# A third set of query and key tiles with loads two heads ahead, and the samples' 8x8 systems inverted on TensorE

## The chip, the cores and the metric

The kernel runs on one NeuronCore of one Trainium2 chip. Its time is the device time of one execution in microseconds (us), and smaller is better. Three runs of the kernel before took 1567.76 to 1576.21 us, with a median of 1574.98 us.

## What is computed

One step of a one-layer decoder for a prompt of 1024 tokens and for 8 samples of 8 tokens each, all float32 in and out:

```
h = rmsnorm(x); P = h @ w_in                      # RWKV columns, then q, k, v
RWKV-7: 8 heads of 64, a recurrence over the tokens, group norm, gate
attention: 8 heads of 64; scores = q k^T / 8 - slope * distance, three
           dilated windows (128,1), (512,4), (2048,16), softmax, @ v; rmsnorm
x = x + concat(rwkv, attention) @ w_out
x = x + top-2 of 8 experts in the best of 4 groups   # 32 gated MLPs of 1024x256
x = x + (p @ w_ple) * sigmoid(rmsnorm(x) @ w_ple_gate); y = rmsnorm(x)
```

The recurrence per head is `s = s*w - (s kk)(kk*a)^T + v k^T`, `y = s r`. In the blocked form it needs, for each block of tokens, the inverse of a unit triangular matrix, T = (I - A)^-1, where A is strictly triangular. For the samples a block is 8 tokens, so A is eight 8x8 blocks on a 64x64 diagonal for each head, and A to the eighth power is zero.

## The kernel before, in words

The program is written as phases on one core, and a scheduler lays the instructions of all phases out on the five engines before the run: each engine then works through its own fixed list in order, and an instruction that waits holds up all that stand behind it in the list. Loads that SyncE (SP) issues also wait for the transfer eight places earlier in its list.

Phase 1 projects all tokens. Phase 2 runs the prompt's recurrence in eight units of 128 tokens, phase 3s the samples' attention over the caches, mixed with phase 2. Phase 3 is the prompt's attention: for each of eight heads and each block `i` of 128 queries, `pS` (q times k, in pieces of 512 keys, L1040), a bias and a maximum on VectorE (L1043), exp on ScalarE (L1052), transposes `pxt` (L1063) and `po` (times v, L1069). Heads 0 and 1 are done in two goes: blocks 0 to 4 in a first call of `phase3`, blocks 5 to 7 in a second, which then does heads 2 to 7 whole. Between the two calls stands the code of phase 2s, the samples' recurrence, whose instructions the scheduler mixes into the attention. Phase 4 multiplies by w_out (`p4y`, L1289) and routes, phase 5 is the experts, phase 6 the end.

A head's k and q come in by `head` (L971, L974): GpSimd (POOL) issues three transfers, k once and q as a high and a low part. The tiles come from the pool `qk3` with two buffers for each name, and `phase3` calls `head` for the unit at hand and the next one. So the load of head h+1 waits until the last `pS` of head h-1 has read its tiles. The bias table of the head (L976, on SP) has two buffers too and is loaded in the same function.

In phase 2s, `prepA` forms the products that hold A in the tile `LAB` (L618) and writes them to memory (`ABs`, L620). `solve_s` (L728) reads the diagonal 8x8 blocks back with eight small loads (L737), inverts all 64 of them by substitution on VectorE (seven pairs of L742 and L744), writes the result into a zeroed array in memory (L748, L750) and reads it back as the tile `TTs` (L752). `sample2` uses `TTs` in `pus` (L820), behind `pst`, `pws` and `pas`.

`attn_out` (L902) takes a finished block of 128 queries: a square with its sum (`asq`, ScalarE, L908), the root on VectorE and POOL (`arm`, `arr`), the scaled rows (`an`, VectorE, L911), four transposes (`pxo`, TensorE, L914), a copy (`ao`, ScalarE, L916) and a store to `MX` (SP, L917), from where phase 4 reads it (L1331). `asq`, `an` and `ao` have one buffer each. The single PSUM bank of `pxo` is used by `p4h`, the routing product of phase 4, after the eighth block.

Of the kernel before, what the change touches and what calls it, by code (L numbers as in the profile page):

```python
# [10 lines left out]
F32 = mybir.dt.float32  # L11
F32R = mybir.dt.float32r
# [9 lines left out]
NP = 1024  # L22
# [438 lines left out]
class K2(K):  # L461
# [10 lines left out]
    def dram2(self):  # L472
        t = lambda n, s: self.dp.tile(s, F32, name=n)
        self.MX = t("MX", [8, 128, T])
        self.ABd = t("ABd", [8, 2, 2, 8, 32, 32])
        self.ABs = t("ABs", [8, 64, 64])
        self.XZ = t("XZ", [8, 64, 64])

    def pools2c(self, es):

# [117 lines left out]
    def prepA(self, u):  # L598

        nc = self.nc  # L600
        smp = u == 's'
        nck, t0, n = (1, NP, 64) if smp else (2, 128 * u, 128)
        ch = self.ch[0 if smp else u // 2 % 2]
        R = lambda t: ch.tile([128, nck, 4, 128], F32, tag=t, name=t)
        G = dict(AR=ch.tile([128, 4, nck, 128], F32, tag="AR", name="AR"), LAB=R("LAB"), Bt=R("Bt"))
        AR, LAB, Bt = G['AR'], G['LAB'], G['Bt']
        c0 = 16 if smp else 2 * u
        nc.sync.dma_start(AR[:, :, 0:nck, :], self.ARd[:, :, c0:c0 + nck, :].rearrange("p k c t -> k p (c t)"))
        bb = self.nxt('bb')
        self.pair_load(bb, self.BB, t0, nck)  # L610
        G['Pc'] = self.pc[:, :, 16:24] if smp else self.pc[:, :, 2 * u:2 * u + 2]
        msk = (self.msks if smp else self.mskp)[:, None, :].to_broadcast([128, 4, 128])
        G['msk'] = msk
        for c in range(nck):
            pg = self.ps("pgb").rearrange("p (i t) -> p i t", i=4)
            for p in range(4):
                nc.tensor.matmul(pg[:, p, :], bb[:, c, p, :], AR[:, p, c, :], start=True, stop=True)
            nc.vector.tensor_tensor(LAB[:, c], pg, msk, op=ALU.mult)  # L618
        if smp:
            nc.sync.dma_start(self.ABs.rearrange("(p h) j t -> (h j) p t", h=2), LAB[:, 0, :, 0:64])  # L620
        else:
            for hh in range(2):
                for b in range(2):
                    q = hh * 64 + b * 32
                    nc.sync.dma_start(self.ABd[u, hh, b].rearrange("s j t -> j s t"),
                                      LAB[q:q + 32].rearrange("p c i t -> p (c i) t")[:, :, 32 * b:32 * b + 32])
        for c in range(nck):
            pg = self.ps("pk").rearrange("p (i t) -> p i t", i=4)
            for p in range(4):
                nc.tensor.transpose(pg[:, p, :], bb[:, c, p, :], self.ident)  # L630
            nc.scalar.activation(Bt[:, c], pg, AF.Copy)
        return G
# [94 lines left out]

    def solve_s(self, G):  # L728

        nc, sv = self.nc, self.sv  # L730
        A8 = sv.tile([64, 8, 8], F32, tag="A8", name="A8")
        X8 = sv.tile([64, 8, 8], F32, tag="X8", name="X8")
        XT8 = sv.tile([64, 8, 8], F32, tag="XT8", name="XT8")
        tmp = sv.tile([64, 64], F32, tag="t8", name="t8")
        diag = lambda d, s: bass.AP(tensor=d.tensor, offset=d[s].offset, ap=[[520, 8], [64, 8], [1, 8]])
        for s in range(8):
            nc.sync.dma_start(A8[8 * s:8 * s + 8], diag(self.ABs, s))  # L737
        nc.gpsimd.memset(X8, 0.0)
        nc.gpsimd.memset(X8.rearrange("p a b -> p (a b)")[:, 0:64:9], 1.0)
        for t in range(1, 8):  # L740
            o = tmp[:, :t * t].rearrange("p (c j) -> p c j", j=t)
            nc.vector.tensor_tensor(o, A8[:, 0:t, t][:, None, :].to_broadcast([64, t, t]),  # L742
                                    X8[:, 0:t, 0:t].rearrange("p j c -> p c j"), op=ALU.mult)
            nc.vector.tensor_reduce(X8[:, t, 0:t], o, axis=AX.X, op=ALU.add)  # L744
        nc.vector.tensor_copy(XT8, X8.rearrange("p t c -> p c t"))
        z = sv.tile([128, 8, 64], F32, tag="tms", name="z8", bufs=2)
        nc.gpsimd.memset(z, 0.0)
        nc.sync.dma_start(self.XZ.rearrange("s m k -> m s k"), z[0:64])  # L748
        for s in range(8):
            nc.sync.dma_start(diag(self.XZ, s), XT8[8 * s:8 * s + 8])  # L750
        TT = G['TT'] = sv.tile([64, 8, 64], F32, tag="TTs", name="TTs")
        nc.sync.dma_start(TT, self.XZ.rearrange("s m k -> m s k"))  # L752

    def chain(self, u, G, y):
        nc, e2 = self.nc, self.e2
# [142 lines left out]
class K3(K2):  # L898
    def dram3(self):
        self.ATS = self.dp.tile([NS, 512], F32, name="ATS")  # L900

    def attn_out(self, pool, X, at, n, i0, gat, tags=("asq", "an", "ao"), bufs=1, w=512):  # L902

        nc = self.nc
        t = lambda i: pool.tile([128, w], F32, tag=tags[i], name=("asq", "an", "ao")[i], bufs=bufs)[:, 0:512]
# [45 lines left out]
    def setup_s(self, es):  # L951
        c3 = es.enter_context(self.pool("c3", side="left"))
        self.gat = c3.tile([128, 512], F32, name="gat")
        self.nc.sync.dma_start(self.gat, self.bcast_row(self.I['attn_gain'], 512))
        self.os = c3.tile([128, 8, 128], F32, name="os")

    def setup(self, es):
        c3 = es.enter_context(self.pool("c3b", side="left"))
        self.at = c3.tile([128, 8, 512], F32, name="at")
        self.qk = es.enter_context(self.pool("qk3", 2, side="left"))  # L960
        self.heads = {}

    def head(self, h, ia, ib):

# [5 lines left out]
        k = self.qk.tile([128, NP], F32R, tag="k", name="k3")  # L970
        nc.gpsimd.dma_start(k[:, :w], dup(self.KP, h * 64, 512 * NP, 0, w))  # L971
        q = self.qk.tile([128, 2, NP], F32R, tag="q", name="q3")
        for a in range(2):
            nc.gpsimd.dma_start(q[:, a, 128 * ia:w], dup(self.QP[a:a + 1], h * 64, 0, 128 * ia, w))  # L974
        bias = self.qk.tile([128, NP], F32, tag="bias", name="bias")
        nc.sync.dma_start(bias[:, NP - w:], self.I['abase'][h][:, NP - w:])  # L976
        self.heads[h, ia] = k, q, bias

    def samples_out(self, pool, X, n, w):

# [13 lines left out]
    def phase3(self, pairs, depth, banks, hooks={}):  # L994
        nc, tc, I, O = self.nc, self.tc, self.I, self.O
        gat, at = self.gat, self.at
        with ExitStack() as es:
# [16 lines left out]
            for p, ia, ib in pairs:  # L1014
# [859 lines left out]
```

## Time and profile before

| what | value |
|---|---|
| median of three runs | 1574.98 us |
| the profiled execution, its own time | 1571.74 us |
| its span from first to last instruction | 1570.0 us |
| mean granted TensorE clock | 0.940 of 2.4 GHz |
| TensorE busy | 1382.5 us, 88% of the span |
| VectorE, ScalarE, POOL busy | 960.4, 738.1, 369.8 us |

The profile is of one execution. Its rows give for a stretch, a line or an instruction how long an engine was busy, how long it stood idle before, and what it waited for then. A granted clock of 1.00 is 2.4 GHz and 0.50 is 1.2 GHz; values between are means over a stretch that had both.

### The profile page before, as it was taken

The numbers are of one execution on the slowest core, as the hardware profiler recorded it, in microseconds if no ns is written. First come the engines' busy times: TensorE is split into PE (matmuls) and PEld (weight loads), VectorE is DVE, ScalarE is ACT, GpSimd is POOL, SyncE is SP. The second block draws the span as 40 slices with busy tenths as digits, with TensorE's granted clock in tenths as the row PEclk, the third lists the DMA queues.
The fourth block names the chain that finished last, engine by engine and source line by source line (L and its number), as shares of the span: only waits on it lengthen the run. The fifth ranks groups of instructions, "written<-read, shape, count | busy, mean of one in ns | idle before, by whom it ended". The sixth has DMA issues, their size and how long they took to land. (4 is left out here: it accounts for less than half of the span.)

```text
span 1570.0 us, 24571 instructions
## 1 busy us (share of the span) xinstructions
PE 1382.5 (88%) x9017; PEld 1152.6 (73%) x9018; DVE 960.4 (61%) x2155; ACT 738.1 (47%) x1336; POOL 369.8 (24%) x362
## 2 busy tenths in 40 slices
PE   4899999999898998975679899995999789899996
PEld 4888999999777776754568678784777566567874
DVE  7524573462287686444457563567988678786664
ACT  5544453221334444522345463243878668783322
POOL 8104453000122223242122351112221101002231
PEclk9999999999898999987889899997999989999998
DMA  6145658896775675255586647558999999997552
GB/s 207 52 156 177 181 154 262 288 353 222 218 216 150 176 190 154 69 120 142 128 255 214 171 128 258 198 212 272 377 391 381 378 332 332 353 379 251 181 173 67
DMA packets 257005, 350.01 MB, mean 223 GB/s; under 512 B 105757, under 2 KB 184415, under 8 KB 256352
## 3 DMA queue, kind: packets, MB, share of 16 engines
q1 hardware_dynamic: 212272, 287.46, 56.0%
q0 software_dynamic: 39712, 43.76, 9.9%
q10 hardware_dynamic: 4896, 17.17, 2.9%
q8 instruction: 73, 1.20, 0.3%
q14 instruction: 52, 0.43, 0.1%
HBM read 277.45 MB, written 104.33 MB: 243 GB/s over the span
## 5 line engine op out<-in xcount | busy, mean ns | idle before, releaser
L264 PE MATMUL pj<-hT_hi,wh 128*128 128x384 f32 (+1 forms) x600 | 199.5, 334 | 4.7 <-DVE lora L272 2.7
L264 PE MATMUL pj<-hT_hi,wl 128*128 128x384 f32 (+1 forms) x600 | 199.1, 332 | 0.0
L264 PE MATMUL pj<-hT_lo,wh 128*128 128x384 f32 (+1 forms) x600 | 198.4, 331 | 0.0
L264 PEld LDWEIGHTS pj<-hT_hi,wh 128*128 128x128 f32 x600 | 114.0, 191 | 6.6 <-DVE lora L272 3.0
L264 PEld LDWEIGHTS pj<-hT_hi,wl 128*128 128x128 f32 x600 | 114.0, 190 | 2.4 <-issue 2.2
L264 PEld LDWEIGHTS pj<-hT_lo,wh 128*128 128x128 f32 x600 | 114.4, 191 | 0.6 <-issue 0.2
L1532 POOL DMA_INDIRECT x<-HN,idx x32 | 49.9, 1560 | 255.2 <-PE p4t L1542 154.1
L49 DVE TENSOR_TENSOR dl<-draw,dh 128x1024 fp32r<-128x1024 f32 x66 | 78.0, 1221 | 43.8 <-ACT dh L47 43.6
L1040 PE MATMUL pS<-k,q 128*128 128x512 f32 (+2 forms) x192 | 55.7, 397 | 37.9 <-DMA q<-QP 36.5
L688 DVE TENSOR_TENSOR ftmp<-At,X 128x60 f32<-128x60 f32 (+24 forms) x248 | 59.7, 252 | 44.1 <-DMA At<-ABd 33.5
L1069 PEld LDWEIGHTS po<-v,pt 128*128 128x128 f32 x576 | 74.5, 198 | 11.0 <-issue 2.7
L1069 PE MATMUL po<-v,pt 128*128 128x128 f32 x576 | 80.0, 284 | 1.6 <-ACT pt L1067 1.3
L1052 ACT ACTIVATE s<-s,nm 128x128 f32<-128x128 f32 (+7 forms) x64 | 49.4, 772 | 62.7 <-DVE X L744 21.5
L47 ACT ACTIVATE dh<-draw 128x1024 fp32r<-128x1024 f32 x66 | 66.2, 1052 | 22.9 <-DMA draw<-in_w_down_dram 13.5
L1040 PEld LDWEIGHTS pS<-k,q 128*128 128x128 f32 x192 | 32.2, 206 | 44.2 <-issue 31.9
L1043 DVE CUSTOM_DVE_ANT_0 s<-pS,bias 128x512 f32<-128x512 f32 (+2 forms) x96 | 50.8, 551 | 19.5 <-PE pxt L1063 15.9
L49 DVE TENSOR_TENSOR wl<-w,wh 128x1024 fp32r<-128x1024 f32 x25 | 35.0, 1400 | 44.6 <-ACT wh L47 43.8
L690 DVE TENSOR_TENSOR X<-X,ftmp 128x60 f32<-128x60 f32 (+24 forms) x248 | 58.7, 248 | 4.5
L1067 ACT ACTIVATE pt<-pxt 128x512 f32<-128x512 f32 (+3 forms) x64 | 32.6, 512 | 58.9 <-PE pxt L1063 44.1
L767 POOL TENSOR_TENSOR s<-S,pc 128x512 f32<-128x512 f32 x16 | 16.9, 1055 | 161.9 <-PE pj L264 70.6
L1289 PE MATMUL p4y<-dh,hh 128*96 128x512 f32 x128 | 46.9, 407 | 7.5 <-ACT hh L47 7.5
L1289 PE MATMUL p4y<-dh,hl 128*96 128x512 f32 x128 | 51.3, 401 | 1.3 <-DVE hl L49 1.3
(653 smaller groups left out, 3793.4 us busy)
## 6 DMA issues: line engine op xcount, KB each, us to landing
wraw<-in_w_gate_dram SPq DMA_DIRECT2D x64, 512.0 KB
wraw<-in_w_up_dram SPq DMA_DIRECT2D x64, 512.0 KB
draw<-in_w_down_dram SPq DMA_DIRECT2D x32, 1024.0 KB
out_dram<-in_cache_k_win_dram SPq DMA_DIRECT2D x16, 1016.0 KB
out_dram<-in_cache_v_win_dram SPq DMA_DIRECT2D x16, 1016.0 KB
w<-in_w_in_dram SPq DMA_DIRECT2D x25, 512.0 KB
kc<-in_cache_k_win_dram SPq DMA_DIRECT2D x48, 256.0 KB
vc<-in_cache_v_win_dram SPq DMA_DIRECT2D x48, 256.0 KB
```

The costliest lines, as they stand in the source:

```text
L47: (hi_eng or nc.scalar).activation(hi, src, AF.Copy) if (hi_eng or nc.scalar) is nc.scalar else hi_eng.tensor_copy(hi, src)
L49: return e.tensor_tensor(lo, src, hi.bitcast(F32), op=ALU.subtract)
L264: nc.tensor.matmul(p[:, :nn], a[:, k, :], b[:, k, n0:n0 + nn], start=(m == 0), stop=(m == 23))
L688: nc.vector.tensor_tensor(o, At[:, t, t + 1:32][:, :, None].to_broadcast([128, m, c]), X[:, t, None, 0:c].to_broadcast([128, m, c]), op=AL ...
L690: nc.vector.tensor_tensor(X[:, t + 1:32, 0:c], X[:, t + 1:32, 0:c], o, op=ALU.add)
L1040: nc.tensor.matmul(ps[:, :n], q[:, a, i * 128:(i + 1) * 128], k[:, c0:c0 + n], start=(a == 0), stop=(a == 1))
L1043: nc.vector.tensor_tensor_reduce(s[:, c0:c0 + n], ps[:, :n], bias[:, bo:bo + n], 1.0, -3e38, ALU.add, ALU.max, m)
L1052: ex = nc.scalar.activation(s[:, :nb * 128], s[:, :nb * 128], AF.Exp, bias=nm, accum_out=den)
L1067: nc.scalar.activation(pt[:, b0:b0 + m, :], px[:, :m, :], AF.Copy)
L1069: nc.tensor.matmul(po, pt[:, b, :], v[:, b, :], start=(b == 0), stop=(b == nb - 1))
L1289: self.nc.tensor.matmul(p, a[x][:, k, :], w, start=(k == 0 and q == 0), stop=(k == kn - 1 and q == 2))
L1532: nc.gpsimd.indirect_dma_start(out=X[e][:n], out_offset=None, in_=self.HN, in_offset=bass.IndirectOffsetOnAxis(ap=self.idx[:, e:e + 1], ax ...
```

## The change

A third set of tiles for k and q comes from a new pool `qx3`, for heads 2 and 5. `phase3` calls `head` for the unit at hand and the next two, and the bias loads become a function of their own, one unit ahead as before. `solve_s` takes A from `LAB` without memory: two ScalarE copies and four transposes give A and its transpose for all eight heads, then 8 products of 64x64 each for A squared, its transpose, A cubed, A to the fourth (transposed), and the last product (I+A+A^2+A^3) A^4; 40 in all, in four steps with copies and sums between them. The arrays `ABs` and `XZ` are gone. In `attn_out`, `asq` shares its buffer with `ao`, and the tile `os` moves to another pool.

```diff
-        self.ABs = t("ABs", [8, 64, 64])
-        self.XZ = t("XZ", [8, 64, 64])
@@ prepA
-        if smp:
-            nc.sync.dma_start(self.ABs.rearrange("(p h) j t -> (h j) p t", h=2), LAB[:, 0, :, 0:64])
-        else:
+        if not smp:
@@ solve_s
-        A8 = sv.tile([64, 8, 8], F32, tag="A8", name="A8")
...
-            nc.sync.dma_start(A8[8 * s:8 * s + 8], diag(self.ABs, s))
...
-            nc.vector.tensor_tensor(o, A8[:, 0:t, t][:, None, :].to_broadcast([64, t, t]),
-                                    X8[:, 0:t, 0:t].rearrange("p j c -> p c j"), op=ALU.mult)
-            nc.vector.tensor_reduce(X8[:, t, 0:t], o, axis=AX.X, op=ALU.add)
...
-            nc.sync.dma_start(diag(self.XZ, s), XT8[8 * s:8 * s + 8])
+        A = G['LAB'][:, 0, :, 0:64]
+        V = lambda t: sv.tile([64, 8, 64], F32, tag=t, name=t)
+        bank = lambda n: self.ps(n).rearrange("p (s k) -> p s k", k=64)
+        lo, hi = slice(0, 64), slice(64, 128)
+        A0, AT, P2, P2T, P4T, R = (V(t) for t in ("sA0", "sAT", "sP2", "sP2T", "sP4T", "sR"))
+        for hh in range(2):
+            nc.scalar.activation(A0.rearrange("p (q h) k -> p q h k", h=2)[:, :, hh], A[hh * 64:hh * 64 + 64], AF.Copy)
+        p = self.ps("pta")
+        for q in range(4):
+            nc.tensor.transpose(p[lo, q * 128:(q + 1) * 128], A[:, q, :], self.ident)
+        nc.vector.tensor_copy(AT.rearrange("p s k -> p (s k)"), p[lo])
+        nc.vector.tensor_tensor(R, A0, self.ident[lo, None, lo].to_broadcast([64, 8, 64]), op=ALU.add)
+
+        def mm(p, r, x, y):
+            for s in range(8):
+                nc.tensor.matmul(p[r, s, :], x[:, s, :], y[:, s, :], start=True, stop=True)
+        p = bank("pp2")
+        mm(p, lo, AT, A0)
+        mm(p, hi, A0, AT)
+        nc.vector.tensor_copy(P2, p[lo])
+        nc.scalar.activation(P2T, p[hi], AF.Copy)
+        p = bank("pp3")
+        mm(p, lo, AT, P2)
+        mm(p, hi, P2, P2T)
+        nc.vector.tensor_tensor(R, R, P2, op=ALU.add)
+        nc.scalar.activation(P4T, p[hi], AF.Copy)
+        nc.vector.tensor_tensor(R, p[lo], R, op=ALU.add)
+        p = bank("pp4")
+        mm(p, lo, P4T, R)
         TT = G['TT'] = sv.tile([64, 8, 64], F32, tag="TTs", name="TTs")
-        nc.sync.dma_start(TT, self.XZ.rearrange("s m k -> m s k"))
+        nc.vector.tensor_tensor(TT, p[lo], R, op=ALU.add)
@@ attn_out
-    def attn_out(self, pool, X, at, n, i0, gat, tags=("asq", "an", "ao"), bufs=1, w=512):
+    def attn_out(self, pool, X, at, n, i0, gat, tags=("ao", "an", "ao"), bufs=1, w=512):
@@ phase123
                 self.head(h, 5, 8)
+                self.bias(h, 5, 8)
+            self.qx = ea.enter_context(self.pool("qx3", side="left"))
@@ head
+        qk = self.qk if h % 3 < 2 else self.qx
+        k = qk.tile([128, NP], F32R, tag="k", name="k3")
...
+        q = qk.tile([128, 2, NP], F32R, tag="q", name="q3")
@@ phase3
-                    self.head(h, ia, ib)
-                    u = units.index((h, ia, ib)) + 1
-                    if u < len(units):
-                        self.head(*units[u])
+                    u = units.index((h, ia, ib))
+                    for w in units[u:u + (3 if len(pairs) > 1 else 2)]:
+                        self.head(*w)
+                    for w in units[u:u + 2]:
+                        self.bias(*w)
```

Three places show how the fixed lists move. The first is POOL's list in the second call of phase 3; the rows with k and q are the loads of one head, `ux` belongs to the samples' recurrence. Before, from the load of head 2 to that of head 4:

```order
L971 DMA k_8057<-KP 128x1x1024 [waits DMASW6_49,PE_49]
L974 DMA q_8059<-QP 128x1x1024 [waits DMASW7_49,DMASW0_49]
L974 DMA q_8059<-QP 128x1x1024
L971 DMA k_8179<-KP 128x1x1024 [waits DMASW1_49,PE_49]
L974 DMA q_8181<-QP 128x1x1024 [waits DMASW3_49,DMASW2_49]
L974 DMA q_8181<-QP 128x1x1024
L832 TENSOR_TENSOR ux<-us,cst 64x512 [waits DMAHW7_49,DVE_49]
L832 TENSOR_TENSOR ux<-us,cst 64x512
L836 TENSOR_TENSOR ST<-ST,pc_110 128x512 [waits DVE_49,Pool_49]
L971 DMA k_8426<-KP 128x1x1024 [waits DMASW4_49,PE_49]
```

After, from the load of head 2, the first from the new pool, to that of head 4:

```order
L981 DMA k_7965<-KP 128x1x1024 [waits DMAHW3_49,DMAHW2_49,DMAHW4_49,PE_49,Activation_49]
L984 DMA q_7967<-QP 128x1x1024 [waits DMAHW4_49,DVE_49,Activation_49]
L984 DMA q_7967<-QP 128x1x1024 [waits DMASW6_49]
L981 DMA k_8085<-KP 128x1x1024 [waits DMASW7_49,PE_49]
L984 DMA q_8087<-QP 128x1x1024 [waits DMASW0_49]
L984 DMA q_8087<-QP 128x1x1024 [waits DMASW1_49]
L838 TENSOR_TENSOR ux<-vt_99,cst 64x512 [waits DVE_49]
L838 TENSOR_TENSOR ux<-vt_99,cst 64x512 [waits Pool_49]
L981 DMA k_8207<-KP 128x1x1024 [waits DMASW2_49,PE_49]
```

Before, the loads of heads 2 and 3 stand behind the first `ux` pair and that of head 4 behind the second; now heads 2 and 3 stand ahead of the first pair, and head 4 right behind it. The load of head 2 no longer waits for a slot of `qk3` but for the last users of the space that `qx3` takes over.

The second place is TensorE's list at the end of the first call of phase 3. Before, between the last `po` of that call and the first `pS` of head 0's blocks 5 to 7:

```order
L1063 MATMUL pxt<-ident,s_7523 128x128 [waits PE_49]
L1063 MATMUL pxt<-ident,s_7523 128x128 x3
L812 MATMUL pws<-ST,AR 128x512 [waits Activation_49]
L1063 MATMUL pxt<-ident,s_7523 128x128 [waits DVE_49,Activation_49]
L1069 MATMUL po<-v_7267,pt 128x128 [waits DVE_49]
L1069 MATMUL po<-v_7267,pt 128x128 x3
L812 MATMUL pws<-ST,AR 128x512 [waits DVE_49]
L1069 MATMUL po<-v_7267,pt 128x128 [waits DVE_49]
L817 MATMUL pas<-vt_101,LAK 128x128 [waits DVE_49,Pool_49]
L1040 MATMUL pS<-k_7567,q_7569 128x512 [waits DMASW7_49,DMASW6_49,DVE_49]
L1040 MATMUL pS<-k_7567,q_7569 128x512 [waits DMASW0_49]
```

After, from the second of the four products on; `pp_7657`, `pp_7676` and `pp_7696` are the banks of the powers, `sA`, `sP2`, `sP4T` and `sR` the tiles of `solve_s`:

```order
L1079 MATMUL pxt<-ident,s_7521 128x128 [waits PE_49]
L1079 MATMUL pxt<-ident,s_7521 128x128 x3
L743 MATMUL pp_7676<-sP_7644,sAT 64x64 [waits Activation_49]
L743 MATMUL pp_7676<-sP_7644,sAT 64x64 x7
L743 MATMUL pp_7676<-sP2T,sP_7644 64x64 x8
L1079 MATMUL pxt<-ident,s_7521 128x128 [waits Activation_49]
L1085 MATMUL po<-v_7265,pt 128x128 x4
L1085 MATMUL po<-v_7265,pt 128x128 [waits DVE_49]
L743 MATMUL pp_7696<-sR,sP4T 64x64 [waits DVE_49]
L743 MATMUL pp_7696<-sR,sP4T 64x64 x7
L1056 MATMUL pS<-k_7565,q_7567 128x512 [waits DMASW7_49,DMASW6_49,DVE_49]
L1056 MATMUL pS<-k_7565,q_7567 128x512 [waits DMASW0_49]
```

The products of `solve_s` now stand between the last groups of `pxt` and `po`, and the last eight directly ahead of head 0's `pS`. `pws` and `pas`, which stood ahead of that `pS`, now come behind it.

The third place is TensorE's list at the last of the eight blocks of `attn_out`, in phase 4; `p4t` belongs to the routing. Before, up to the eighth `pxo`:

```order
L1371 MATMUL p4t<-ident,xa 128x128 [waits DMAHW7_49]
L1371 MATMUL p4t<-ident,xa 128x128 x3
L1371 MATMUL p4t<-ident,xa 128x128 [waits DVE_49]
L1371 MATMUL p4t<-ident,xa 128x128 x3
L1289 MATMUL p4y<-whz,mh 128x512
L1289 MATMUL p4y<-whz,ml 128x512
L1289 MATMUL p4y<-wlz,mh 128x512
L1289 MATMUL p4y<-whz,mh 128x512
L1289 MATMUL p4y<-whz,ml 128x512
L1289 MATMUL p4y<-wlz,mh 128x512
L914 MATMUL pxo<-ident,an 128x128 [waits DVE_49,Activation_49]
L914 MATMUL pxo<-ident,an 128x128 x3
```

After, at the sixth, seventh and eighth `pxo` and the first `p4h` that takes over their bank:

```order
L1305 MATMUL p4y<-why,mh 128x512
L920 MATMUL pxo<-ident,an 128x128 [waits DVE_49,Activation_49]
L920 MATMUL pxo<-ident,an 128x128 x3
L1305 MATMUL p4y<-why,ml 128x512
L1305 MATMUL p4y<-wly,mh 128x512
L920 MATMUL pxo<-ident,an 128x128 [waits DVE_49,Activation_49]
L920 MATMUL pxo<-ident,an 128x128 x3
L920 MATMUL pxo<-ident,an 128x128 [waits DVE_49,Activation_49]
L920 MATMUL pxo<-ident,an 128x128 x3
L1396 MATMUL p4h<-wrt,ht 64x36 [waits DMAHW2_49,DMAHW0_49,Activation_49]
L1396 MATMUL p4h<-wrt,ht 64x36 x7
```

Before, fifteen `p4y` (the last six are shown) and the `p4t` stood between the seventh `pxo` and the eighth; now two `p4y` stand between the sixth and the seventh `pxo`, and none between the seventh and the eighth.

## Rows read from the trace of the kernel before

**Rows 1.** Windows (stretch us; each engine's busy us; PEclk, DMA share, GB/s): the experts.

```profile
1100.00:1200.00 100.00, 100.00 (x508) 72.00 (x506) 89.32 (x114) 82.84 (x125) 22.93 (x11) 1.00 1.03 386
```

**Rows 2.** Waits of TensorE, 640 to 940 us: total, times, longest.

```profile
PE pS L1040 <- DMA q<-QP: 36.5, 6, 15.2
```

**Rows 3.** Timeline of TensorE: start, us, engine, line, [idle before <-releaser].

```profile
740.28 0.55 PE L817 MATMUL pas<-vt,LAK 128*128 128x128 f32 x1 [14.60 <-DVE X L744]
...
768.00 0.44 PE L1040 MATMUL pS<-k,q 128*128 128x128 f32 x1 [15.21 <-DMA q<-QP]
...
817.00 0.66 PE L1040 MATMUL pS<-k,q 128*128 128x128 f32 x2 [8.32 <-DMA q<-QP]
...
865.51 0.30 PE L1040 MATMUL pS<-k,q 128*128 128x128 f32 x1 [1.33 <-DMA q<-QP]
...
870.22 0.48 PE L1040 MATMUL pS<-k,q 128*128 128x128 f32 x1 [4.41 <-DMA q<-QP]
```

**Rows 4.** Timeline of VectorE and of SP's queue at the inversion.

```profile
738.21 0.15 DVE L742 TENSOR_TENSOR t<-A,X 64x1 f32<-64x1 f32 x1 [14.22 <-DMA s0s<-in_state_wkv_dram]
...
728.70 5.33 SPq L737 DMA_DIRECT2D A<-ABs  x4
```

**Rows 5.** Windows of three stretches: clock after each wait.

```profile
740.30:744.30 4.00, 4.00 (x13) 3.34 (x14) 3.88 (x15) 0.14 (x1) 1.22 (x2) 0.54 0.88 258
...
817.00:823.00 6.00, 6.00 (x17) 3.93 (x18) 2.81 (x10) 1.84 (x3) 0.81 (x1) 0.54 0.97 291
...
870.20:877.20 7.00, 6.98 (x27) 5.88 (x28) 2.91 (x12) 2.44 (x4) 2.08 (x2) 0.51 0.88 284
```

**Rows 6.** Timeline, small products and transposes on TensorE, copy on VectorE.

```profile
664.29 1.83 PE L713 MATMUL px<-R,LAB 32*32 32x32 f32 x32
...
668.62 0.63 PE L723 MATMUL px<-RT,X 32*32 32x32 f32 x32
...
710.64 0.60 PE L630 MATMUL pk<-ident,bb 128*128 128x128 f32 x4
...
707.88 0.68 DVE L577 COPY so<-pS 128x512 f32<-128x512 f32 x1
```

**Rows 7.** Timeline of POOL at two heads' loads, and the tile q's landing times.

```profile
746.00 1.59 POOL L974 DMA_DIRECT2D q<-QP  x2
...
788.84 0.84 POOL L971 DMA_DIRECT2D k<-KP  x1 [3.27 <-PE pS L1040]
...
DMA to landing us min/median/max: 11.7/19.0/27.2
```

**Rows 8.** Timeline of ScalarE, POOL, VectorE: the links of `attn_out`.

```profile
932.11 0.63 ACT L908 ACTIVATE asq<-at 128x512 f32<-128x512 f32 x1 [0.57 <-DVE at L1070]
...
933.35 0.54 POOL L61 TENSOR_TENSOR arr<-arm,mhalf 128x1 f32<-128x1 f32 x1 [7.06 <-DVE arm L59]
...
936.15 0.75 DVE L911 SCALAR_TENSOR_TENSOR an<-at,arr,gat 128x512 f32<-128x512 f32 x1 [0.99 <-PE pxo L914]
...
938.19 0.58 ACT L916 ACTIVATE ao<-pxo 128x512 f32<-128x512 f32 x1
```

**Rows 9.** Timeline of SP's queue: stores to `MX` and the reads behind them.

```profile
931.08 0.36 SPq L917 DMA_DIRECT2D MX<-ao  x1
...
933.40 0.36 SPq L1331 DMA_DIRECT2D mx<-MX  x1
...
941.83 0.39 SPq L917 DMA_DIRECT2D MX<-ao  x1
...
946.36 0.36 SPq L1331 DMA_DIRECT2D mx<-MX  x1
```

**Rows 10.** Window of the last head beside phase 4; two neighbouring `p4y`.

```profile
915.40:960.70 45.30, 45.30 (x270) 36.56 (x269) 18.05 (x45) 21.28 (x43) 14.52 (x18) 1.00 0.50 144
...
932.51 0.40 PE L1289 MATMUL p4y<-why,ml 128*128 128x512 f32 x1
...
932.74 0.39 PE L1289 MATMUL p4y<-wly,mh 128*128 128x512 f32 x1
```

More of the change, by code (lines that the diff above doesn't have):

```diff
@@ L730, in solve_s @@
         nc, sv = self.nc, self.sv
-        A8 = sv.tile([64, 8, 8], F32, tag="A8", name="A8")
[L732 to L736, printed above, removed]
-            nc.sync.dma_start(A8[8 * s:8 * s + 8], diag(self.ABs, s))
-        nc.gpsimd.memset(X8, 0.0)
@@ L739, in solve_s @@
-        nc.gpsimd.memset(X8.rearrange("p a b -> p (a b)")[:, 0:64:9], 1.0)
-        for t in range(1, 8):
-            o = tmp[:, :t * t].rearrange("p (c j) -> p c j", j=t)
-            nc.vector.tensor_tensor(o, A8[:, 0:t, t][:, None, :].to_broadcast([64, t, t]),
-                                    X8[:, 0:t, 0:t].rearrange("p j c -> p c j"), op=ALU.mult)
-            nc.vector.tensor_reduce(X8[:, t, 0:t], o, axis=AX.X, op=ALU.add)
-        nc.vector.tensor_copy(XT8, X8.rearrange("p t c -> p c t"))
@@ L746, in solve_s @@
[L746 to L749, printed above, removed]
-            nc.sync.dma_start(diag(self.XZ, s), XT8[8 * s:8 * s + 8])
+        A = G['LAB'][:, 0, :, 0:64]
[3 more added lines that the diff above has]
+        A0, AT, P2, P2T, P4T, R = (V(t) for t in ("sA0", "sAT", "sP2", "sP2T", "sP4T", "sR"))
@@ L954, in setup_s @@
         self.nc.sync.dma_start(self.gat, self.bcast_row(self.I['attn_gain'], 512))
-        self.os = c3.tile([128, 8, 128], F32, name="os")
+        self.os = self.e2.tile([128, 8, 128], F32, name="os")
     def setup(self, es):
@@ L960, in setup @@
         self.qk = es.enter_context(self.pool("qk3", 2, side="left"))
-        self.heads = {}
+        self.heads, self.biases = {}, {}
     def head(self, h, ia, ib):
@@ L968, in head, with bias @@
         dup = lambda x, r, step, a, b: bass.AP(tensor=x.tensor, offset=x[0, r:r + 1, a:a + 1].offset, ap=[[step, 2], [NP, 64], [1, b - a]])
-        k = self.qk.tile([128, NP], F32R, tag="k", name="k3")
+        qk = self.qk if h % 3 < 2 else self.qx
+        k = qk.tile([128, NP], F32R, tag="k", name="k3")
         nc.gpsimd.dma_start(k[:, :w], dup(self.KP, h * 64, 512 * NP, 0, w))
-        q = self.qk.tile([128, 2, NP], F32R, tag="q", name="q3")
+        q = qk.tile([128, 2, NP], F32R, tag="q", name="q3")
         for a in range(2):
             nc.gpsimd.dma_start(q[:, a, 128 * ia:w], dup(self.QP[a:a + 1], h * 64, 0, 128 * ia, w))
-        bias = self.qk.tile([128, NP], F32, tag="bias", name="bias")
-        nc.sync.dma_start(bias[:, NP - w:], self.I['abase'][h][:, NP - w:])
-        self.heads[h, ia] = k, q, bias
+        self.heads[h, ia] = k, q
+    def bias(self, h, ia, ib):
+        if (h, ia) in self.biases:
+            return
+        w = 128 * ib
+        bias = self.biases[h, ia] = self.qk.tile([128, NP], F32, tag="bias", name="bias")
+        self.nc.sync.dma_start(bias[:, NP - w:], self.I['abase'][h][:, NP - w:])
     def samples_out(self, pool, X, n, w):
@@ L1021, in phase3 @@
                     n = 128 * ib
-                    self.head(h, ia, ib)
-                    u = units.index((h, ia, ib)) + 1
-                    if u < len(units):
-                        self.head(*units[u])
-                    k, q, bias = self.heads[h, ia]
+                    u = units.index((h, ia, ib))
[3 more added lines that the diff above has]
+                        self.bias(*w)
+                    (k, q), bias = self.heads[h, ia], self.biases[h, ia]
                     if hh == 0:
```

## The prediction, written before the changed kernel ran

> **What bounds the kernel now.** I read the busy shares first: TensorE works 88% of the span, so an edit counts only through the stretches in which TensorE stands idle, and through what it gives TensorE to do. The next view was the windows of 100 us. Behind phase 4 the experts run with TensorE busy for all of 100 us and the DMA engines at a share of 1.03 [rows 1]. That stretch begins when phase 4 hands over and contains nothing that the change touches, so I let a gain or loss ahead of it move the end one to one. The third view was the waits of TensorE in the attention of the prompt: 36.5 us in six waits of `pS` for the load of `q` [rows 2]. Its timeline gives five of the waits that this change can reach [rows 3]: 14.60 us of `pas` for VectorE, then 15.21, 8.32, 1.33 and 4.41 us of `pS` for `q`. (The other 7.2 of the 36.5 us are the first head's, ahead of the place of the change.)
>
> The 14.60 us end with VectorE, but VectorE was itself idle for 14.22 us before the first step of the substitution [rows 4]. The row names the state loads `s0s`; the eight small loads of A are issued behind these on SP, the last four over 5.33 us from 728.70. So it is the way through memory that holds TensorE, not the arithmetic.
>
> **What goes.** (a) The 14.60 us: `solve_s` has no load left, and `pas` no longer stands at the head of the second call. (b) The 15.21 us are head 2's load, issued at 746.00, when the last `pS` of head 0 had freed its buffers, and used at 768.00: 22.0 us [rows 3, 5]. Its new issue point leaves a residue, below. (c) Head 4's load was issued at 788.84 and used at 817.00, 28.2 us later, of which 8.32 were waited; (d) head 6's waits are 1.33 + 4.41 = 5.74 us. The order puts each of these loads one head earlier. A head lasts about 20 us ((817.00 - 768.00 - 8.32) / 2 = 20.3), so the lead grows from 28.2 - 8.3 = 19.9 us to about 40, beyond the longest landing of a `q`, 27.2 us [rows 5]. I take (c) and (d) as gone.
>
> (e) Behind each wait TensorE's granted clock is near 0.5, its level of 1.2 GHz: 0.54 for 4 us, 0.54 for 6 us and 0.51 for 7 us [rows 6]. The loss is 4 x 0.46 + 6 x 0.46 + 7 x 0.49 = 8.0 us, and goes with the waits (a), (c) and (d).
>
> Together -(14.60 + 15.21 + 8.32 + 5.74 + 8.0) = -51.9 us.
>
> **What is added.** (f) The inversion on TensorE is 40 products of 64x64 and four transposes. No row has a product of that size. Thirty-two of 32x32 took 0.63 us in one place and 1.83 us in another, 0.02 to 0.06 us each, and four transposes of 128x128 took 0.60 us, 0.15 us each [rows 7]. So 40 cost 0.8 to 6.0 us; I take 0.07 each, near the larger of the small ones, 2.8 us, and 0.6 for the transposes. The four steps are joined by copies; one of 128x512 takes 0.68 us on VectorE [rows 7]. The order puts `pxt` and `po` between most steps, and only the last eight products stand bare ahead of `pS`, so about 2 us of these hand-offs show. That is +5.4 us, between 2 (all hidden but the products at their fastest) and 11 (products at 0.15 and every step bare).
>
> (r) Head 2's tiles now lie in space that the first call has used, so its load starts only when that call is over, and TensorE then has heads 0 and 1's blocks 5 to 7 to do. Before, this work ran from 740.28 to 768.00 - 15.21 = 752.79, 12.5 us; less 1.8 us of low clock and with some 4 us of the inversion that falls here, 14.7 us. The load takes 22.0 us as before, so 7.3 us of wait remain at head 2. By the landings of `q`, 11.7 to 27.2 us, plus its 1.59 us of issue [rows 5], it is 0 to 14. The value rests on head 2's own row, which had the same neighbours on the queues. The tables and `v` for that stretch now also stand behind the sixteen state loads on SP; the same 0 to 14 us cover them, since they end before head 2's.
>
> (g) `attn_out` pays for the space. `asq` of the next block now waits until the store of `ao` has landed, and so becomes a ring with one block in flight: `asq` 0.63, `arr` 0.54, `an` 0.75, four transposes 0.60, `ao` 0.58 us [rows 7, 8], some 0.9 us of hand-offs and the small `arm`, 4.0 us in sum; then the store. From its issue to the issue of the read behind it passed 2.3 us (931.08 to 933.40) and 4.5 us (941.83 to 946.36) [rows 9]. A period is then 6.3 to 8.5 us; I take 7.2, toward the shorter since the read also waits for its own turn. Does TensorE have as much to do between two `pxo`? In this stretch it is busy in 45.30 of 45.30 us at full clock, and two `p4y` start 0.23 us apart [rows 10]. By the new order 29, 27, 20, 33 and 41 `p4y` stand between the first six `pxo`, and with the attention's products that is 7.5 to 10.0 us each: covered. Between the sixth and the seventh stand two, with the transposes 1.1 us, and between the seventh and the eighth none, 0.6 us. That leaves (7.2 - 1.1) + (7.2 - 0.6) = 12.7 us of idle TensorE, 11 to 15 by the two periods, and I add 2 us of low clock behind two such waits, as in rows 6: +15, in all 12 to 19. The list is fixed, so the `p4y` behind cannot fill it, and `p4h` stands behind the eighth `pxo` and takes its bank. That this price is a loss and not a shift: the routing that it holds up gates the experts.
>
> (h) The loads of the samples' attention and the tile `os` move a few places. I cost that at nothing, since TensorE has other work beside it; by the waits of the first head, the 7.2 us of [rows 2] that lie next to it, it may be 7 us either way. The bias tables, now in a function of their own, come one unit ahead as they did.
>
> **Sum.** -51.9 + 5.4 + 7.3 + 15 = -24.2 us. The profiled execution took 1571.7 us by its own time, so 1547.5. The median of the runs is 3.2 us above it; as the three differ by more than that, I add half: **1549 us**.
>
> The Trainium skill, "DMA: Bandwidth & Descriptors", "Anatomy of one DMA - SWDGE (gpsimd) path", fits a load that POOL issues as 2.0 us plus its bytes over 436 GB/s. By that a `q` half of 512 KB lands in 3.2 us, and the trace disagrees: its shortest landing is 11.7 us [rows 5]. The fit looks at one transfer alone, while the state loads and caches lie beside these. By it the residue (r) would be nothing and the sum -31.5 us.
>
> **Rivals.**
> 1. *The ring of `attn_out` decides (slower).* If a store to `MX` lands late, all seven periods are bare and not two. With a period P the stalls are 7P less the 46.3 us of TensorE's work that lies between the `pxo`, and about 3 us of low clock. They eat up the 39.2 us of the rest from P = 11.8, a landing of 7.8 us; at a landing of 10 us, P = 14, the stalls are 54.7 us and the time about 1589. For it: the loads of `q` take as much on POOL's queue. Against it: the stores' own rows, 2.3 and 4.5 us, and a DMA share of 0.50 in this stretch [rows 9, 10]. Chance 0.08.
> 2. *A third set makes the queue longer, not faster.* With two heads' loads in flight each lands later, and (c) stays with its low clock: 8.3 + 2.8 = 11.1 us, 1560. For it: landing times spread from 11.7 to 27.2 us, which a lone transfer would not. Against it: a lead of 40 us outlasts even the longest. Chance 0.14. The Trainium skill, same page, "Queues, rings and completion order", says that an engine of the DMA takes turns between the queues that have work for it; that speaks for this rival, and no row here shows the turns.
> 3. *The change does not do what it says at (a).* `pS` of head 0, or `pas` one group later, waits for another load behind the state loads on SP; the last of A's loads left SP at 734.0 [rows 4], 8 us after TensorE fell idle, and with 1.8 us of low clock kept this gives 1549 + 10 = 1559. Against it: the order puts 22 `pS` ahead of `pas`. Chance 0.05.
> 4. *`attn_out` is hidden.* If the last `pxo` run late for reasons of the attention anyway, as the ring is then free beforehand, (g) is nothing: 1534. For it: the attention's end, not `p4y`, may set when a block is ready. Chance 0.12.
> 5. *Head 2's load lands in time* (r = 0): 1542. For it: the shortest landing, 11.7 us. Chance 0.09.
>
> **How the numbers follow.** My forecast keeps 0.52. Its own range, from the ends of (f), (r), (g) and (h), is 1538 to 1560. For all cases I take 1531 to 1568: it leaves out rival 1 (0.08), part of rival 4, and the upper tail of rivals 2 and 3, together under 0.2. A measurement tells 0.5%, 7.9 us, from no change: faster is below 1567, slower above 1583. Faster gets 0.52 x 0.95, 0.14 x 0.75, 0.05 x 0.8, and rivals 4 and 5 whole, 0.85; slower gets most of rival 1, 0.07; the rest, 0.08, is the same.
>
> **What would show it.** Right: no wait of TensorE over 2 us between the end of the first call and head 2; one wait for `q` of some 7 us at head 2, and none at heads 4 and 6; the clock at 1.00 where rows 6 have 0.5; two idle stretches of about 6 us ahead of the last two `pxo`, released in the end by ScalarE's `asq` and a store to `MX`. Wrong: waits of 5 us at heads 3 to 7 (rival 2); a `p4y` window with gaps at every `pxo` (rival 1); `solve_s` groups on TensorE that add up to more than 6 us; or a new wait of another engine at the places of rows 3.

## The result and the profile after

The changed kernel is slower, by less than 1% but clear of the noise: 1584.3 us (median of ten runs, 1576.76 to 1589.62) against 1571.53 us (ten runs, 1565.77 to 1577.36), a ratio of 1.0087 [1.0063, 1.0111], where -1.4% was forecast. Its profiled execution was its fastest, 1576.76 us with a span of 1574.4; a second profile, of 1583.25 us, is used below (`e8_after_again`).

One correction: three group numbers in the prediction are shifted. What it calls rows 5 (POOL and the landings) is the group **Rows 7**, its rows 6 (the clock) are **Rows 5**, and its rows 7 (small products) are **Rows 6**. From here on the groups are named by the numbers that they carry.

The first step is to lay milestones of TensorE side by side, from the first and last starts of its groups (us). The stretches between them are what the experiments below are read by.

| profile | first `pS` | last `po` | last `p4y` of w_out | first expert product `dh,hh` | last | span |
|---|---|---|---|---|---|---|
| before | 688.5 | 950.8 | 1057.8 | 1099.3 | 1418.4 | 1570.0 |
| after | 695.8 | 930.0 | 1056.8 | 1097.8 | 1425.6 | 1574.4 |
| after, second profile | 697.9 | 934.3 | 1062.5 | 1103.9 | 1431.7 | 1581.5 |

Against before, the first profile of after loses 7.3 us until the first `pS`, gains 28.1 in the attention (262.3 to 234.2), loses 19.8 from there to the end of w_out (107.0 to 126.8), loses 8.7 in the experts (319.1 to 327.8), and gets 3.3 back elsewhere (0.5 ahead of the experts, 2.8 behind their last product). Together that is +4.4 us of span.

Of the five waits of [rows 3] in the attention four are gone, and head 2's is down to 2.12 us. TensorE's timeline of after (start, duration, engine, line, in brackets the idle time before and who ended it) has these in their place, and behind them one window with its clock:

```profile
741.01 0.77 PE L1056 MATMUL pS<-k,q 128*128 128x512 f32 x1 [3.58 <-DMA q<-QP]
...
744.17 0.80 PE L1056 MATMUL pS<-k,q 128*128 128x512 f32 x1 [2.39 <-DMA q<-QP]
...
752.82 0.80 PE L1056 MATMUL pS<-k,q 128*128 128x512 f32 x1 [1.84 <-DMA q<-QP]
...
767.33 0.33 PE L1056 MATMUL pS<-k,q 128*128 128x128 f32 x1 [2.12 <-DMA q<-QP]
```
```profile
740.00:760.00 20.00, 14.76 (x42) 9.67 (x43) 8.92 (x28) 4.49 (x8) 4.83 (x6) 0.59 0.94 171
```

The first three are not head 2. They come at the start of the second call, for blocks 5 to 7 of heads 0 and 1, whose loads POOL issued at 718.71 and 728.30. Before, `q` of these two landed between 727.3 and 735.7, while TensorE waited 14.60 us for VectorE (725.7 to 740.3). With that wait gone they are late themselves, by 7.8 us. They also took longer: 21.3 to 23.7 and 20.5 to 22.9 us from issue to landing, against 18.7 to 19.2 and 16.1 before; how much of the 7.8 us that makes was not separated. The granted clock is 0.59 over the 20 us, in which TensorE is busy for 14.76, so some 6 us are lost (14.76 x 0.41). Heads 4 and 6 show no wait for `q`. In the second profile the loads of heads 0 and 1 are late by 11.6 us, and head 2 does not wait.

The products of `solve_s`, TensorE's groups of its line (count, shortest/median/longest ns, first and last start):

```profile
L743 PE MATMUL pp<-sA,sAT x16: 218/218/266, 729.7 to 730.6; 64*64 64x64 f32 x16
...
L743 PE MATMUL pp<-sR,sP4T x16: 218/218/267, 736.3 to 737.2; 64*64 64x64 f32 x16
```

Eight products of the code stand as sixteen in the records, from 729.7 to 730.6: 0.06 us for one record and 0.12 for a product. The forty cost some 4.8 us, where 2.8 were taken. The hand-offs between the steps do not show: from the transposes to the first late load TensorE is busy for 9.61 of 9.63 us.

```profile
727.80:737.43 9.63, 9.61 (x119) 8.66 (x118) 4.38 (x12) 3.79 (x7) 3.06 (x4) 1.00 0.80 153
```

In phase 4 the two gaps stand where the prediction put them. First TensorE's timeline at the last three `pxo` and the routing behind them, then ScalarE's and SP's of the links:

```profile
948.33 0.60 PE L920 MATMUL pxo<-ident,an 128*128 128x128 f32 x4
...
954.42 1.09 PE L920 MATMUL pxo<-ident,an 128*128 128x128 f32 x4 [5.03 <-DVE an L917]
...
961.02 1.09 PE L920 MATMUL pxo<-ident,an 128*128 128x128 f32 x4 [5.51 <-DVE an L917]
962.86 1.39 PE L1396 MATMUL p4h<-wrt,ht 128*64 128x36 f32 x11 [0.75 <-ACT ao L922]
...
967.89 3.60 PE L1396 MATMUL p4h<-wrt,ht 128*128 128x36 f32 x16 [3.11 <-DVE lgs L1397]
```
```profile
951.90 0.63 ACT L914 ACTIVATE asq<-at 128x512 f32<-128x512 f32 x1 [2.28 <-DMA MX<-ao]
...
955.61 0.60 ACT L922 ACTIVATE ao<-pxo 128x512 f32<-128x512 f32 x1 [2.98 <-PE pxo L920]
...
958.49 0.63 ACT L914 ACTIVATE asq<-at 128x512 f32<-128x512 f32 x1 [2.29 <-DMA MX<-ao]
```
```profile
949.65 0.36 SPq L923 DMA_DIRECT2D MX<-ao  x1
...
956.23 0.36 SPq L923 DMA_DIRECT2D MX<-ao  x1
```

`asq` ends waits of 2.28 and 2.29 us for the store of `ao`; from `pxo` to `pxo` (954.42 to 961.02) a turn of the ring takes 6.6 us, and `pxo` waits 5.03 and 5.51. Two things more come with it. `p4h` behind the last `pxo` waits 0.75 and 3.11 us, the latter for VectorE's `lgs`; ahead of `lgs` VectorE itself had waited for the load of `gain`, and TensorE's list has no `p4y` here to fill the time:

```profile
965.39 2.05 DVE L1376 SCALAR_TENSOR_TENSOR hn<-xa,r4r,gain 64x1024 f32<-64x1024 f32 x1 [4.52 <-DMA gain<-in_norm_ffn_dram]
```

The other is the clock:

```profile
948.00:972.00 24.00, 9.60 (x53) 8.18 (x52) 6.05 (x10) 5.47 (x11) 2.55 (x7) 0.63 0.51 158
972.00:980.00 8.00, 8.00 (x42) 6.85 (x40) 2.46 (x3) 1.24 (x3) 1.13 (x2) 0.83 1.00 369
```

In 24 us TensorE is busy for 9.60 (idle 14.4), at 0.63 over the stretch, and 0.83 over the 8 behind it. With 14.4 us idle and some 5 us of low clock (0.37 x 9.6 + 0.17 x 8 = 4.9) this is 19.3 of the 19.8 us. The kernel before had 2.9 us of idle time of its own in its 107.0 us, at the routing, at a mean clock of 0.97.

In the experts TensorE's longest wait is where all engines meet at the test for overflow of an expert. For each kernel, before first: the branch on SP and on VectorE (line, queue, operation, duration ns, start), what TensorE waited there, and SP's loads around it.

```profile
L1647 DVEq COMPARE_BRANCH  x1: 72/72/72, 1350.2 to 1350.2; - x1
L1647 SPq COMPARE_BRANCH  x1: 50/50/50, 1342.1 to 1342.1; - x1
  PE p4g L1289: 6.1, 1
...
1341.62 0.42 SPq L1247 DMA_DIRECT2D wraw<-in_w_up_dram  x1
1352.78 0.39 SPq L1271 DMA_DIRECT2D draw<-in_w_down_dram  x1
```
```profile
L1663 DVEq COMPARE_BRANCH  x1: 72/72/72, 1350.9 to 1350.9; - x1
L1663 SPq COMPARE_BRANCH  x1: 53/53/53, 1352.4 to 1352.4; - x1
  PE p4g L1305: 8.7, 1
```
```profile
1340.18 0.38 SPq L1287 DMA_DIRECT2D draw<-in_w_down_dram  x1
1352.06 0.33 SPq L1262 DMA_DIRECT2D wraw<-in_w_gate_dram  x1
1356.00 0.39 SPq L1287 DMA_DIRECT2D draw<-in_w_down_dram  x1
```

Before, SP reaches the branch 8 us ahead of VectorE, after its load of `w_up` at 1341.62. After, one more load of `w_gate` stands ahead of the branch in SP's list. It can go only at 1352.06, and SP is last. The next load leaves at 1356.00, 5.1 us behind VectorE's branch; before it left at 1352.78, 2.6 us behind. From 1340 to 1380 TensorE is busy for 27.7 us, before for 33.9. The late loads show behind the branch: ScalarE waits for one of `w_up`, its `xh` comes late, and TensorE waits 2.12 and 1.47 us where before it did not wait.

```profile
1370.46 2.01 ACT L47 ACTIVATE whc<-wraw 128x1024 fp32r<-128x1024 f32 x2 [2.28 <-DMA wraw<-in_w_up_dram]
...
1375.06 0.47 PE L1305 MATMUL p4g<-whc,xh 128*96 128x512 f32 x1 [2.12 <-ACT xh L47]
...
1376.99 0.36 PE L1581 MATMUL p4h<-ident,h 96*128 96x96 f32 x2 [1.47 <-DVE h L1573]
```

That is 3.6 of the 8.7 us. The wait at the branch itself is 2.6 us longer, but it ended ahead of SP's branch, so SP's lateness did not lengthen it. The rest is longer busy time (296.1 us against 292.6, at a clock of 0.95 and 0.96), less 1.0 us of other waits. No line of the diff touches the experts: the scheduler laid their instructions out anew.

### The profile page after: what moved, and what is told of

It reads as the page before. It is cut to its first block, busy times and chain, and to the rows that moved or that the text cites. A ratio compares the mean times of both kernels' runs of the same rounds, so it can differ in the third digit from the quotient of the medians.

```text
span 1574.4 us, 24700 instructions
## 1 busy us (share of the span) xinstructions
PE 1400.5 (89%) x9101; PEld 1168.0 (74%) x9102; DVE 961.1 (61%) x2146; ACT 741.7 (47%) x1340; POOL 368.1 (23%) x359
## 5 line engine op out<-in xcount | busy, mean ns | idle before, releaser
L1059 DVE CUSTOM_DVE_ANT_0 s<-pS,bias 128x512 f32<-128x512 f32 (+2 forms) x96 | 50.8, 551 | 12.7 <-PE pS L1056 10.7
L1305 PE MATMUL p4y<-dl,hh 128*96 128x512 f32 x128 | 51.3, 401 | 0.0
```

Of the source, the lines that this page charges most:

```text
L1059: nc.vector.tensor_tensor_reduce(s[:, c0:c0 + n], ps[:, :n], bias[:, bo:bo + n], 1.0, -3e38, ALU.add, ALU.max, m)
L1305: self.nc.tensor.matmul(p, a[x][:, k, :], w, start=(k == 0 and q == 0), stop=(k == kn - 1 and q == 2))
```

## The experiments

Ratios are to the kernel before, run on the same chip, with a 95% interval.

**`e1_own`**: the changed kernel with

```diff
-tags=("ao", "an", "ao")
+tags=("asq", "an", "ao")
```

> The changed kernel with a buffer of its own for `asq` again, nothing else. The trace of the changed kernel shows two losses that I had not sized right: phase 4 loses 19.8 us between the end of the attention and the last `p4y` of w_out (where the attention ended 20.8 us earlier than before, w_out ends only 1.0 us earlier), and the experts lose 8.7 us. Theory: the 19.8 us are the ring asq-ao-store. Then this kernel takes 1584 - 20 = 1564 us, no `pxo` waits over 2 us, and the experts stay as in the changed kernel, since SP's list of the experts' loads keeps the changed kernel's order up to the branch of the overflow test. Rival: phase 4 is held by something else that follows the attention's end (the reads of MX, the routing), and the time stays at 1584, with the same idle time at other lines.

Measured: 1559.53 us, 0.9945 [0.9921, 0.9968]. From the last `po` to the last `p4y` 101.4 us (126.8 with the shared buffer), no idle time at the last two `pxo`:

```profile
935.10 0.60 PE L920 MATMUL pxo<-ident,an 128*128 128x128 f32 x4
...
942.14 0.60 PE L920 MATMUL pxo<-ident,an 128*128 128x128 f32 x4
```
```profile
935.00:1036.40 101.40, 101.40 (x570) 86.20 (x569) 60.23 (x139) 35.11 (x53) 13.16 (x26) 1.00 0.66 232
```

This shows the shared buffer to be the cause of phase 4's loss. Against this kernel it costs 25.4 us, more than the 19.8 against the kernel before, as phase 4 here has no idle time at all. Its list of the experts' loads ends at the branch like that of after, and they took 331.0 us. Space was no reason for the shared buffer: with `os` moved, the kernel fits without it.

**`e2_an`**: `tags=("an", "an", "ao")` in the same place.

> The changed kernel with `asq` sharing its buffer with `an` instead of `ao`, so that no store stands in the ring. This also puts the experts' loads back into the order of the kernel before as far as the branch (`... gu | d gu` in place of `... gud | gu`). Theory A (ring 19.8 us, and the experts' 8.7 us are the place of the branch in SP's list): 1584 - 20 - 9 = 1555 us, TensorE idle at the branch by some 3 us less, the experts' end as far behind their start as in the kernel before (319 us from the first to the last `dh,hh` product, 328 in the changed kernel). Theory B (the experts' loss is chance from run to run): as the kernel with a buffer of its own, 1564 us. Rival: 1584, as there.

Measured: 1560.22 us, 0.9944 [0.9920, 0.9968]. The experts took 317.6 us, as theory A said. But phase 4 took 114.0 us, 12.6 more than with a buffer of its own. No `pxo` waits; TensorE stands idle for 7.5 us, 5.7 of them at the `p4h` behind the last `pxo`, where in `e1_own` it has other work:

```profile
949.65 1.12 PE L1396 MATMUL p4h<-wrt,ht 128*64 128x36 f32 x16 [0.73 <-ACT ao L922]
955.73 3.60 PE L1396 MATMUL p4h<-wrt,ht 128*128 128x36 f32 x16 [4.95 <-DVE lgs L1397]
```

Whether the shorter ring or the new order of the list makes this was not separated. Against `e1_own` the loss in phase 4 and the gain in the experts cancel.

**`e3_share`**: the kernel before with `tags=("ao", "an", "ao")` alone.

> The kernel before with nothing but `asq` sharing the buffer of `ao`. Its list of the experts' loads is that of the changed kernel. Theory: both losses come from this one edit, +20 for the ring and +9 for the experts' order: 1571.5 + 29 = 1600 us. Rival 1: the ring costs only its two last waits, as the prediction said, +15 (1587), or +12 without its low clock. Rival 2: experts' loss is chance: 1591. Rival 3: the ring costs nothing without the earlier end of the attention: 1572.

Measured: 1595.72 us, 1.0179 [1.0152, 1.0207], or +28 us. Phase 4 took 123.5 us (107.0), the experts 325.4 (319.1), but the attention 251.4 (262.3), with a wait of 8.23 us at head 2. The profile is of its fastest execution, 1587.73 us, so it shows only 16 of the 28 us. One line of the change costs twice what the whole of it lost.

**`e4_solve`**: the kernel before with the new `solve_s` and the lines of `prepA` that go with it; two sets of k and q, `os` and `asq` as before.

> The kernel before with the new `solve_s` alone: two sets of k and q, `asq` with its own buffer, `os` where it was. Theory: the 14.6 us wait of `pas` and its 1.8 us of low clock go, 5 us of products and hand-offs come; the 15.2 us of head 2 stay, as its load starts when head 0's last `pS` is done, which moves with the rest: 1571.5 - 11 = 1560 us. Rival: the wait only moves to another load behind the state loads on SP, or head 2's wait grows by what `pas` gave back: 1572. The experts' list has a third order here (`dgugugudgu` earlier on), so up to 9 us either way may come from there; the trace's first and last expert products tell it.

Measured: 1553.99 us, 0.9914 [0.9883, 0.9945]. The 15.2 us of head 2 are gone too, which I had expected to stay. TensorE's waits over 2 us between 720 and 920:

```profile
736.04 0.76 PE L1046 MATMUL pS<-k,q 128*128 128x512 f32 x1 [4.62 <-DMA q<-QP]
...
739.22 0.79 PE L1046 MATMUL pS<-k,q 128*128 128x512 f32 x1 [2.42 <-DMA q<-QP]
...
797.63 0.69 PE L1046 MATMUL pS<-k,q 128*128 128x128 f32 x2 [4.88 <-DMA q<-QP]
...
849.94 0.47 PE L1046 MATMUL pS<-k,q 128*128 128x128 f32 x1 [4.80 <-DMA q<-QP]
```

Head 2's load left POOL at 731.72, not 745.17: it waits for `pS` of head 0, and that had waited with the rest of TensorE behind `pas`. The first two waits are head 1's blocks 5 to 7: the loads that come out late in after do so with two sets as well. The attention took 236.9 us, against 234.2 and 236.4 in the two profiles of after, with the third set.

**`e5_third`**: all of the change but `solve_s` (the one through memory stays) and `tags` (as before).

> The kernel before with the third set of k and q, the loads two heads ahead, the bias function and `os` in its new pool, but with the old `solve_s` through memory and with `asq` in its own buffer. Theory: the third set only shortens waits for `q` (29.3 us in the kernel before at heads 2, 4 and 6, of which the new `solve_s` alone left 9.7 at heads 4 and 6, in rows of two new waits of 4.88 and 4.80), the 14.6 us of `pas` stay, and the moves ahead of the first head cost some 7 us: 1568.5 - 25 + 7 = 1551 us. Rival: with the inversion still on SP's queue head 2's load lands late as before and takes back half of it, 1560; or, as the third set does nothing that the new `solve_s` doesn't, 1568 + 7 = 1575.

Measured: 1574.48 us, 1.0019 [0.9996, 1.0043], nearest to the second rival. Two waits of 16 us stay, one now at `po`, and one for head 2 in spite of its third set:

```profile
751.00 0.58 PE L1079 MATMUL po<-v,pt 128*128 128x128 f32 x1 [16.68 <-ACT pt L1077]
...
788.58 0.87 PE L1050 MATMUL pS<-k,q 128*128 128x128 f32 x2 [16.53 <-DMA q<-QP]
```

**`e6_os`**: the kernel before with

```diff
-        self.os = c3.tile([128, 8, 128], F32, name="os")
+        self.os = self.e2.tile([128, 8, 128], F32, name="os")
```

> The kernel before with nothing but the tile `os` moved to the other pool, as in the change. Theory: this alone costs the 6 to 10 us by which the first `pS` is late in the three kernels that have the change's third set (695.8, 698.6 and 695.0 us, against 688.5), since `os` then comes to lie where the recurrence's tiles of phase 2 are still in use: first `pS` at 695 or later, 1575 us. Rival: the delay comes from the order in which the scheduler now mixes phase 3s, set by the other edits (the bias function, the two-ahead calls); then the first `pS` is at 688.5 and the time 1568.

Measured: 1580.91 us, 1.0064 [1.0036, 1.0092], or +10 us (6 to 14), and the first `pS` at 696.2 (688.5 before). The theory holds for the cost. Its reason is not shown: the edit changes the order of the lists in phases 2 and 3s (the first `kc` and `vc` loads go ahead of `sb`, `qs` and `ks` on SP), and I did not separate order from place.

**`e7_solve_q3`**: `e4_solve` with a third buffer for `q` alone, in the pool `qx3`:

```diff
+        q = (self.qk if h % 3 < 2 else self.qx).tile([128, 2, NP], F32R, tag="q", name="q3")
...
+                    if len(pairs) > 1 and u + 1 < len(units):
+                        self.loadq(*units[u + 1])
```

> The new `solve_s` with a third buffer for `q` alone (k keeps two), `q` loaded two heads ahead, `os` and `asq` where they were in the kernel before. Theory: this takes the q waits of heads 4 and 6 that are left with the new `solve_s` alone (4.9 and 4.8 us and some low clock behind them) without the moves ahead of the first head: 1554 - 8 = 1546 us, the best of all. Rival: k's load, which still waits for the last `pS` of the head two before, lands as late as `q` did, and the time stays at 1554.

Measured: 1558.48 us, 0.9923 [0.9896, 0.9950], no better than `e4_solve`. As the rival said, k is late now: one wait of 5.62 us for `k<-KP` at 810.08.

**`e8_after_again`**: the changed kernel, unedited.

> The changed kernel once more, unedited, for a second profile: the first one was of its fastest run (1576.8 us, the median is 1584.3). Theory: the 8 us between lie in the stretch where the DMA engines are the limit, the experts (327.8 us from the first to the last `dh,hh` product in the first profile), since everything ahead of it waits for compute: this profile, if it is of a slower run, shows the experts longer and the rest as before to 2 us. Rival: the attention's waits for `q` vary, and the stretch from the first `pS` to the last `po` (234.2 us) is longer instead.

Measured: 1583.25 us. The experts took 327.8 us in both profiles, so the theory was wrong. The 7 us are spread: 2.1 until the first `pS`, 2.2 in the attention, 1.4 in phase 4, the rest around the experts.

**`e9_solve_dve`**: `e4_solve` with

```diff
-            nc.scalar.activation(A0.rearrange(...)[:, :, hh], A[hh * 64:hh * 64 + 64], AF.Copy)
+            nc.vector.tensor_copy(A0.rearrange(...)[:, :, hh], A[hh * 64:hh * 64 + 64])
```

> The new `solve_s` alone, as in the kernel of that name, but with the two copies of A from `LAB` on VectorE instead of ScalarE. The edit itself is worth under 1 us. It also puts SP's list of the experts' loads into the same order as in the kernel with only `os` moved and the one with `asq` sharing with `an`, whose experts took 317.7 and 317.6 us from the first to the last `dh,hh` product; with the order of the kernel with the new `solve_s` alone two kernels took 324.7 and 324.7. Theory: the experts' time goes with the order of that list: here 318 us (322 at most, as in the kernel with a third buffer for `q`), and 1554 - 6 = 1548 us. Rival: the experts' time goes with when they start or with chance, and stays near 325 and 1554.

**`e10_solve_again`**: `e4_solve`, unedited.

> The new `solve_s` alone once more, unedited, beside the kernel with the copies on VectorE on one chip: a second profile of the list that gave 324.7 us in the experts. Theory: 325 again to 1.5 us, and a time 6 us above the kernel with the copies on VectorE. Rival: the two are equal within their interval.

Measured, `e9_solve_dve` first: 1550.13 us, 0.9878 [0.9848, 0.9909], and 1555.69 us, 0.9909 [0.9879, 0.9938]. The experts took 317.2 us and 327.6. The spans of the two profiles are only 2.8 us apart all the same, as `e9_solve_dve` loses 5.0 us in the attention and 1.7 ahead of it. The times differ as expected, by 5.6 us, though their intervals overlap; the 327.6 lie 1.1 us beyond what I had allowed for a repeat. Over all twelve profiles the experts' time goes with the order of SP's list around the branch: 327.8, 327.8, 331.0 and 325.4 us where the extra load stands ahead of it; 317.6, 317.7 and 317.2 in one other order (and 322.1 where only the loads behind the experts differ from it); 319.1 in that of before; 324.7, 324.7 and 327.6 in that of `e4_solve`. In all four of the first group TensorE waits for `xh` behind the branch (1.1 to 2.8 us), in none of the other eight; this explains a part of their loss. The rest of it, and why the last group is slower with SP early at the branch, stay open.

`e9_solve_dve` has the lowest ratio of all: the new `solve_s`, with its two copies moved to VectorE, and nothing else of the change.

## Why the prediction was wrong

Forecast: -24 us (-51.9 + 5.4 + 7.3 + 15). Measured: +12.8 in the medians. Taken alone, the parts of the change are `solve_s` -0.9%, `os` +0.6%, the shared buffer +1.8%, and the third set some -0.5% (`e5_third` less `e6_os`), in sum +1.1%, near the 0.9% measured together. Taken out of the whole change (`e1_own`), the shared buffer is worth 1.4%.

- **(a), rival 3.** The 14.60 us went. What I did not ask was which loads that wait had hidden: those of heads 0 and 1's blocks 5 to 7 came out from behind it, 7.8 us late. Rival 3 named the place, though with a load on SP, and gave it 0.05.
- **(b) and (r).** Head 2's 15.21 us were no fault of two buffers. They were the same wait a second time, since its load was issued behind `pas` through `pS`. So the third set could win only (c) and (d), and the new `solve_s` alone left 4.88 and 4.80 of these. As to size, the residue was forecast at 7.3 us and measured at 2.1, in the second profile at nothing. That is luck: head 2's second `q` load took 27.7 us, not 22.0, but the stretch ahead of it, taken as 14.7 us, lasted 27.8 (737.4 to 765.2) with its waits and low clock.
- **(c), (d).** Right, the two went; rival 2 did not come at heads 4 and 6, though the landings of `q` did lengthen (median 19.0 to 21.4 us), and at heads 0 and 1 that adds to the waits of (a).
- **(e).** Half right: the clock is at 1.00 behind heads 4 and 6, but at 0.59 at the start of the second call, some 6 us that the sum had as gone.
- **(f).** Right in sum, by luck: a product took 0.12 us and not 0.07, 2 us more in all, and the 2 us of hand-offs did not show.
- **(g).** The place, the mechanism and the period (6.6 us, 7.2 taken) were right, the price too small: 19.8 us, not 15, and 25.4 against `e1_own`. The two waits were 10.5 us, less than the 12.7 taken; `p4h` behind the ring (3.9 us) and the clock (4.9, not 2) made the rest. The order showed `p4h` directly behind; I used it only as what fills the bank.
- **(h).** This step failed. "I cost that at nothing" was measured at +0.64% for `os` alone, some 10 us; in the changed kernel the first `pS` is 7.3 us late, at the edge of its bounds of 7.
- **"I let a gain or loss ahead of it move the end one to one."** This step failed as well: the experts took 8.7 us more. Their list was laid out anew, and rows tie 3.6 of the 8.7 us to SP's loads behind the branch. The order of the changed kernel shows the move; I looked only at the places that the diff names.

The sum, by the first profile's span: 28.6 us lie between -24.2 and +4.4. The attention gave 28.1 us where the terms (a) to (f) and (r) make 39.2; of these 11 us the waits of heads 0 and 1 and the low clock of (e) are 14, less 5 from (r), and some 2 lie in small waits that I did not single out. (g) is 5 us, (h) 7 and the experts 9, less the 3.3 that came back elsewhere. Another 8 us lie between that profile and the median of after; the second profile has 7 of them, spread over the program. The range left out a case in which several places lose at once: one edit of `attn_out` was worth +28 us, as much as the gain in the attention.

The Trainium skill's fit for a POOL load ("DMA: Bandwidth & Descriptors", "Anatomy of one DMA - SWDGE (gpsimd) path") is no better borne out after: by it 512 KB land in an estimated 3.2 us, and the shortest landing of `q` is 11.8 us, the median 21.4.

## What to carry to other kernels

Before paying for deeper buffers, take the first wait of a chain away by itself: loads behind it are issued late because of it, and look like a shortage of buffers. Ask also which loads were hidden in that wait, as they are late next. A buffer shared to make room closes a ring, and its price is the period less the work listed between its turns; check the bytes first, here the room was there. Where a scheduler lays out the whole program, compare the lists of every stage that sets the time, also of those which the diff does not touch.

## What the runs showed of the hardware

Eight float32 products of 64x64 stood as sixteen records that started 0.06 us apart. The granted clock was 0.59 on average over 20 us in which TensorE was busy three quarters of the time in short pieces. The loads of `q` landed in 21.4 us in the median with three sets and with two in 19.0 (before) and 17.8 (`e4_solve`); the shortest and longest are alike (11.8 and 27.7, 11.7 and 27.2, 12.4 and 25.6).
